# Diagonal blocks that stay in SBUF around a triangular solve, and engine queues re-planned from a table of durations, in a hybrid DeltaNet and attention layer

## The chip, the cores and the metric

The kernel runs on one core of one Trainium2 chip. The metric is the device time of one execution in microseconds; the time of a kernel is the median over several executions. Five queues matter: PE (TensorE, matrix products), DVE (VectorE), ACT (ScalarE), POOL (GpSimd), and SP (SyncE), which in this kernel only issues DMAs. Each engine takes its instructions strictly in the order of its own queue. An instruction whose inputs are not there stops everything behind it on that engine.

## The reference

One layer over 2048 tokens of width 1024, all in fp32. The input is normalised and projected, and the columns of the projection feed two groups of heads. Group A (four heads of 128) is a gated DeltaNet, run forward and backward over the sequence. Group B (eight query heads of 64) is attention in a window of 128 with a sink. Both pass a gate, and one output projection adds the result to the input. What the change touches is the DeltaNet:

```python
m = jnp.where(strict, jnp.einsum('bhncd,bhnsd->bhncs', k_beta, k) * decay, 0.0)
t_inv = lax.linalg.triangular_solve(eye + m, eye, left_side=True, lower=True, unit_diagonal=True)
u = jnp.einsum('bhncs,bhnse->bhnce', t_inv, v * beta[..., None])
...
def step(state, inp):               # scanned over the chunks, forward and backward
    v_new = u_i - jnp.einsum('bhcd,bhde->bhce', w_i, state)
    o = einsum(q_i * exp(g_i), state) + einsum(a_i, v_new)
    state = state * exp(g_last) + einsum(k_dec, v_new)
```

In each chunk and direction a unit triangular matrix is inverted, and the inverses feed a recurrence over the chunks.

## The kernel before

The kernel works in chunks of 128 tokens (16 of them, `NCH`). fp32 operands of the large projections are split into a high and a low fp32r part, so that such a product is three matmuls.

- **Phase A** normalises and transposes the input and runs all projections with the convolution and the attention. Products are `pq_*` (rows), `pf_c*` (convolution) and `pf_z*` (gates); attention products are `s`, `pt`, `po`.
- **Phase B** takes the four DeltaNet heads h = 0 to 3, each in four functions. `pre_front(h)` loads keys and queries of four chunks at a time (`k_q`), transposes them (`tr`, `trv`), forms the products `gh` and writes the scaled triangular matrices `ma` (tiles `ma`, and for some heads `xhi_h` and `xlo_h`). `solve(h)` inverts the 32x32 diagonal blocks of all 16 chunks and both directions at once: each of the 128 partitions holds one block, `L` has the blocks and `X` their inverses, and 31 steps of two dependent DVE instructions each (lines 749 and 753) do the elimination. `invert(h)` builds the 128x128 inverses from the blocks in four groups `hi`, each with five matmul products `pi0` to `pi4`; it places the small inverses in the tiles `iv0` to `iv3` and in `ma`. `scan(h)` is the recurrence: 16 steps, two directions, products `pk`, `py`, `po`, states `S`, and at its end a normalisation (`sso`, `tro`, `zt`) into DRAM (`mix_dn`).
- **Filling work** in phase B is `sw_units`: 32 units `pcs` that project the attention outputs (loads `mxs`, `xrs`, `zcs`, stores `part`). In the end `out_pair` projects the DeltaNet outputs (`pcd`).

The blocks travel between these functions through DRAM. After each group of four chunks, `pre_front` stores the matrices with a DMA to `m_d` (line 716). `solve` loads the diagonal blocks back with two DMAs, `X` for the forward half (line 739) and `L` for the backward half (line 740); DVE copies the forward half into `L` transposed (line 742), and POOL clears `X`. After the last step `X` is stored to `x_d` (line 754). `invert` loads `xc` from there, one DMA for each group and direction (line 765), and DVE transposes 32x32 blocks of it into `xt` (line 766); copies on DVE or POOL (lines 776 and 793) put both in place.

The order of all instructions on each engine is not that of the code. `set_order` builds a graph of dependences over all instructions, gives every instruction a duration (`cost`) and every dependence a delay (`LAG`), and plans the queues by list scheduling, forward and backward in turn, 12 times (`plan`). The plan with the shortest end is written out as the order of each queue. A DMA has a fixed issue time, one landing delay for loads and stores alike (`LAG` of SP) and a transfer time worked out from its pieces; the durations of the other engines come from formulas in the number of elements.

Of the kernel before, what the change touches and what calls it, by code (L numbers as in the profile page):

```python
# [7 lines left out]
F32 = mybir.dt.float32  # L8
# [7 lines left out]
P = 128  # L16
# [530 lines left out]
def phase_b(ctx, wide, xe, ae, late, tc, t, ident, consts, hp, mix_dn, mix_sw, kq_d, v_d, zdn_d, zsw_d, dp, out):  # L547
# [93 lines left out]
    def pre_front(h):  # L641
# [10 lines left out]
        m_d = dp.tile([2, NCH, 4 * (32 * P + 32)], F32, tag="m_d", name=f"m_d{h}", bufs=2)  # L652
        x_d = dp.tile([2, NCH, P, 32], F32, tag="x_d", name=f"x_d{h}", bufs=2)
        for n, c4 in enumerate(FRONT):
# [60 lines left out]
            for d in range(2):  # L715
                dma(m_d[d, s4, : P * P].rearrange("u (i j) -> i u j", j=P), ma[d, c4][:, :, 0])
# [13 lines left out]
        H["solve"] = m_d, x_d, mp  # L730
        return H

    def solve(h, H):
        m_d, x_d, _ = H["solve"]
        L = qa.tile([P, 32, 32], F32, tag="L", name=f"L{h}")
        X = qa.tile([P, 32, 32], F32, tag="X", name=f"X{h}")
        lv = [m_d[d].rearrange("u (p y) -> (u p) y", p=4)[:, : 32 * P] for d in range(2)]
        lv = [a.rearrange("q (r x) -> q r x", x=P)[:, :, :32] for a in lv]
        dma(X[0:64], lv[0])
        dma(L[64:128], lv[1])  # L740
        x = X.rearrange("p r c -> p (r c)")
        V.tensor_copy(L[0:64], X[0:64].rearrange("p r c -> p c r"))
# [11 lines left out]
        dma(x_d.rearrange("d u (p r) c -> (d u p) (r c)", p=4), X.rearrange("p r c -> p (r c)"))  # L754

    def invert(h, H):
        _, x_d, mp = H["solve"]
        for hi in range(4):
# [3 lines left out]
            for d, c4 in ((0, hi), (1, 3 - hi)):  # L762
                xc = qb.tile([P, 4, 32], F32, tag="xc", name=f"xc{h}_{d}_{c4}", bufs=4)
                xt = qb.tile([P, 4, 32], F32, tag="xt", name=f"xt{h}_{d}_{c4}", bufs=4)
                dma(xc, x_d[d, 4 * c4 : 4 * c4 + 4].rearrange("u i c -> i u c"))
                V.transpose(xt.rearrange("p u c -> p (u c)"), xc.rearrange("p u c -> p (u c)"))
                x0[d], x1[d] = (xc, xt) if d == 0 else (xt, xc)
# [277 lines left out]
def set_order(tc):  # L1045
# [371 lines left out]
```

## Time and profile before

| quantity | value |
|---|---|
| median of three timed executions | 1261.1 us |
| lowest and highest of them | 1256.62 and 1261.7 us |
| profiled execution, span from first to last instruction (the only time shown for it) | 1268.0 us |
| mean granted TensorE clock over the span | 0.989 |
| PE busy | 1210.5 us (95%), 7018 instructions |
| DVE busy | 953.7 us (75%), 2320 instructions |
| ACT busy | 725.8 us (57%) |
| POOL busy | 529.2 us (42%) |
| DMA | 206.39 MB, 163 GB/s in the mean |

The profile is of one execution. An instruction row gives start, duration, engine, line, operation, names of output and inputs, shape, and in brackets how long its engine sat idle before it and what ended that. A row of windows gives, for a stretch of time, its length, the busy time of PE, PE's weight load, DVE, ACT and POOL with the number of their instructions, the granted TensorE clock, the share of the DMA engines and GB/s. A fp32 matmul is two PE instructions. The ends of matmuls are modelled, so that a PE that is called busy may still be running below its best rate.

### The profile page before, as it was taken

Reading aid. Unit: us, or ns where it says so; the run is one execution under the profiler, and the core shown is the slowest. Engines: PE = TensorE matmul, PEld = TensorE weight load, DVE = VectorE, ACT = ScalarE, POOL = GpSimd, SP = SyncE. Lnnn points to the kernel's source line nnn. Section 1 sums busy time; section 2 is a strip of 40 time slices with the busy share of each in tenths; the row PEclk is TensorE's granted clock in tenths of the full one; section 3 lists DMA queues with packets and bytes.
Section 4 is the critical chain, followed back from the end, with each engine's and each line's share of the span. In section 5 each row is a group of like instructions: output and inputs, shape, how many; then the busy total and the mean of one; then the engine's idle time right before and its main releaser. Section 6 shows DMA issues by size and latency. Waiting matters only on the chain.

```text
span 1268.0 us, 22351 instructions
## 1 busy us (share of the span) xinstructions
PE 1210.5 (95%) x7018; PEld 1037.4 (82%) x7018; DVE 953.7 (75%) x2320; ACT 725.8 (57%) x2167; POOL 529.2 (42%) x845
## 2 busy tenths in 40 slices
PE   6999999999999999999999998999889899999898
PEld 5998888788889988887777777888789689888776
DVE  4523689999854379999995587698769779876765
ACT  6432476666534367766665438658557845685421
POOL 2243454763302276556422304613742441670541
PEclk9999999999999999999999999999889999999999
DMA  7553243513544434431016848967955875854785
GB/s 259 172 160 125 75 154 100 173 60 102 166 145 125 144 110 137 137 96 55 34 51 207 238 141 245 264 189 207 268 166 174 236 200 152 242 175 122 238 269 199
DMA packets 232294, 206.39 MB, mean 163 GB/s; under 512 B 49137, under 2 KB 181873, under 8 KB 232177
## 3 DMA queue, kind: packets, MB, share of 16 engines
q1 hardware_dynamic: 232176, 204.97, 53.0%
q8 instruction: 56, 0.92, 0.3%
q14 instruction: 62, 0.50, 0.1%
HBM read 139.84 MB, written 65.08 MB: 162 GB/s over the span
## 4 chain that ended last, share of the span: by engine, by line
PE 67%; DVE 13%; DMA 9%; ACT 4%; issue 3%; POOL 1%; SPq 1%; DVEq 0%; ACTq 0%; POOLq 0%
PE pf_c L199 5%; PE pf_c L201 5%; PE pf_c L200 5%; PE pf_z L199 4%; PE pf_z L200 4%; PE pf_z L201 4%; PE pi L781 3%; PE pq_q L212 2%; PE pq_q L211 2%; PE pt L390 2%; PE pq_q L210 2%; DMA xc<-x_d 2%; PE py L830 2%; PE po L839 2%; PE pcs L596 2%
## 5 line engine op out<-in xcount | busy, mean ns | idle before, releaser
L199 PE MATMUL pf_c<-xhi,wh_c 128*128 128x512 f32 x384 | 155.7, 405 | 0.8 <-DVE acc L269 0.8
L200 PE MATMUL pf_c<-xlo,wh_c 128*128 128x512 f32 x384 | 154.7, 403 | 0.0
L201 PE MATMUL pf_c<-xhi,wl_c 128*128 128x512 f32 x384 | 154.3, 402 | 0.0
L269 DVE SCALAR_TENSOR_TENSOR acc<-pf_c,cw,acc 128x512 f32<-128x512 f32 (+1 forms) x192 | 140.8, 742 | 2.6 <-POOL acc L259 0.7
L385 POOL TENSOR_SCALAR pr<-pr,st 128x384 f32<-128x384 f32 (+1 forms) x128 | 79.4, 639 | 98.0 <-DVE st L383 71.2
L394 ACT ACTIVATE ph<-pt 128x512 fp32r<-128x512 f32 x92 | 53.0, 595 | 60.5 <-PE pt L390 51.5
L376 ACT ACTIVATE pr<-pr,st 128x384 f32<-128x384 f32 (+1 forms) x128 | 76.2, 597 | 17.8 <-DVE st L372 17.4
L199 PEld LDWEIGHTS pf_c<-xhi,wh_c 128*128 128x128 f32 x384 | 72.5, 189 | 13.5 <-DVE acc L269 1.3
L201 PEld LDWEIGHTS pf_c<-xhi,wl_c 128*128 128x128 f32 x384 | 72.3, 188 | 12.9
L200 PEld LDWEIGHTS pf_c<-xlo,wh_c 128*128 128x128 f32 x384 | 72.4, 188 | 11.6
L835 ACT ACTIVATE yk<-py,ck 128x128 f32<-128x128 f32 x120 | 43.9, 366 | 62.0 <-PE py L830 61.2
L372 DVE CUSTOM_DVE_ANT_0 pr<-s,mask,sink 128x384 f32<-128x384 f32 (+1 forms) x128 | 73.4, 593 | 2.5 <-PE s L371 1.0
L211 PE MATMUL pq_q<-wh_q,xlo 128*128 128x256 f32 x256 | 72.1, 282 | 0.0
L212 PE MATMUL pq_q<-wl_q,xhi 128*128 128x256 f32 x256 | 71.9, 281 | 0.0
L210 PE MATMUL pq_q<-wh_q,xhi 128*128 128x256 f32 x256 | 71.4, 280 | 0.0
L390 PE MATMUL pt<-ident,pr 128*128 128x128 f32 x368 | 69.5, 274 | 1.8 <-DVE pl L395 1.1
L395 DVE TENSOR_TENSOR pl<-pt,ph 128x512 fp32r<-128x512 f32 x92 | 61.6, 681 | 6.1 <-ACT ph L394 5.6
L390 PEld LDWEIGHTS pt<-ident,pr 128*128 128x128 f32 x368 | 47.8, 140 | 20.4 <-DVE pl L395 4.4
L596 PE MATMUL pcs<-wohs,mhs 128*128 128x512 f32 x128 | 58.3, 456 | 4.4 <-ACT mhs L590 2.7
L692 POOL TENSOR_TENSOR nk<-ssk,pw 128x4 f32<-128x4 f32 x16 | 16.5, 1029 | 106.8 <-DVE ssk L691 106.6
L597 PE MATMUL pcs<-wohs,mls 128*128 128x512 f32 x128 | 56.1, 438 | 1.7 <-DVE mls L591 1.7
L598 PE MATMUL pcs<-wols,mhs 128*128 128x512 f32 x128 | 55.0, 429 | 0.0
(324 smaller groups left out, 4029.4 us busy)
## 6 DMA issues: line engine op xcount, KB each, us to landing
kqc<-kq_d SPq DMA_DIRECT2D x120, 128.0 KB, 3.1
ws_c<-wt SPq DMA_DIRECT2D x48, 256.0 KB, 3.5
xr<-x SPq DMA_DIRECT2D x16, 512.0 KB, 5.3
k_q<-kq_d SPq DMA_DIRECT2D x16, 512.0 KB, 5.6
mxs<-mix_sw SPq DMA_DIRECT2D x32, 256.0 KB, 3.7
xrs<-x SPq DMA_DIRECT2D x32, 256.0 KB, 3.7
part<-xrs SPq DMA_DIRECT2D x32, 256.0 KB, 2.6
xrd<-part SPq DMA_DIRECT2D x32, 256.0 KB, 4.1
```

The source lines that it names most:

```text
L199: T.matmul(ps, hi[:, k, cs], xhi[b][:, k], start=(k == 0), stop=False)
L200: T.matmul(ps, hi[:, k, cs], xlo[b][:, k], start=False, stop=False)
L201: T.matmul(ps, lo[:, k, cs], xhi[b][:, k], start=False, stop=(k == KC - 1))
L210: T.matmul(ps[:, :n], xh, hi[:, k, :n], start=(k == 0), stop=False)
L211: T.matmul(ps[:, :n], xl, hi[:, k, :n], start=False, stop=False)
L212: T.matmul(ps[:, :n], xh, lo[:, k, :n], start=False, stop=(k == KC - 1))
L269: V.scalar_tensor_tensor(av, ps[:, lo:], cw[:, i, k : k + 1], av, ALU.mult, ALU.add)
L372: V.tensor_tensor_reduce(pr[j][:, :n], ps[:, :n], mask[:, lo * P : hi * P], 1.0, sink[:, hh : hh + 1], ALU.add, ALU.min, accum_out=nm[:, j ...
L376: A.activation(pr[j][:, :n], pr[j][:, :n], AF.Exp, bias=nm[:, j : j + 1], scale=-1.0, accum_out=den[:, j : j + 1])
L385: G.tensor_scalar(pr[j][:, :n], pr[j][:, :n], den[:, j : j + 1], 1.0, ALU.mult, ALU.mult)
L390: T.transpose(pt[:, j], pr[j][:, (kb - lo) * P : (kb - lo + 1) * P], ident)
L596: T.matmul(ps, mh[:, k], wh[:, k], start=(k == 0), stop=False)
```

## The change

It has two parts. The first keeps the blocks in SBUF. `pre_front` copies each diagonal block with POOL from `ma` into one of two tiles (`C` and `L`, named `Cg` and `Lg` in the order's rows): 32 copies of 32x128 elements for each head. `solve` transposes the backward half into `C` (512 elements on each partition) and the whole into `L` (1024 elements) with DVE's 32x32 transpose, and after the 31 steps transposes `X` twice (1024 elements each) into `XC` and `XT`, from which `invert` takes slices. The tiles `Cg` and `XC` share one buffer (tag `C`), and `Lg`, `L` and `XT` share another (tag `L`). All DMAs to and from `m_d` and `x_d` are gone.

The second part changes the planner. Durations come from a table of means (`TIMES`, by engine, names and number of elements), transfer times of DMAs from another (`MOVES`); a landing takes `LOAD` for a load into SBUF and `STORE` for a store, plus the transfer. The search runs twice, with a smaller and a larger time spared after every DMA. Candidates are no longer compared by the planned end but by the mean end of three replays (`replay`), in which the queue orders stay fixed, durations vary at random, DMAs land late by a random amount, and 3 in 100 DMA issues take longer. This moves instructions everywhere in the program.

```diff
-        m_d = dp.tile([2, NCH, 4 * (32 * P + 32)], F32, tag="m_d", name=f"m_d{h}", bufs=2)
-        x_d = dp.tile([2, NCH, P, 32], F32, tag="x_d", name=f"x_d{h}", bufs=2)
+        blocks = [qa.tile([P, n, 32], F32, tag=k, name=f"{k}g{h}") for k, n in (("C", 32), ("L", 16))]
...
             for d in range(2):
-                dma(m_d[d, s4, : P * P].rearrange("u (i j) -> i u j", j=P), ma[d, c4][:, :, 0])
+                for q in quads:
+                    G.tensor_copy(blocks[d][q, s4], ma[d, c4][q, :, 0, q])
...
     def solve(h, H):
-        m_d, x_d, _ = H["solve"]
+        C, B = H["solve"][0]
+        V.transpose(C[:, NCH:].rearrange("p u r -> p (u r)"), B.rearrange("p u r -> p (u r)"))
         L = qa.tile([P, 32, 32], F32, tag="L", name=f"L{h}")
         X = qa.tile([P, 32, 32], F32, tag="X", name=f"X{h}")
-        lv = [m_d[d].rearrange("u (p y) -> (u p) y", p=4)[:, : 32 * P] for d in range(2)]
-        lv = [a.rearrange("q (r x) -> q r x", x=P)[:, :, :32] for a in lv]
-        dma(X[0:64], lv[0])
-        dma(L[64:128], lv[1])
+        V.transpose(L, C.rearrange("p u r -> p r u"))
         x = X.rearrange("p r c -> p (r c)")
-        V.tensor_copy(L[0:64], X[0:64].rearrange("p r c -> p c r"))
...
-        dma(x_d.rearrange("d u (p r) c -> (d u p) (r c)", p=4), X.rearrange("p r c -> p (r c)"))
+        XC = qa.tile([P, 32, 32], F32, tag="C", name=f"XC{h}")
+        XT = qa.tile([P, 32, 32], F32, tag="L", name=f"XT{h}")
+        V.transpose(XC.rearrange("p u c -> p c u"), X.rearrange("p r c -> p c r"))
+        V.transpose(XT.rearrange("p u r -> p r u"), X)
+        H["solved"] = XC, XT
...
             for d, c4 in ((0, hi), (1, 3 - hi)):
-                xc = qb.tile([P, 4, 32], F32, tag="xc", name=f"xc{h}_{d}_{c4}", bufs=4)
-                xt = qb.tile([P, 4, 32], F32, tag="xt", name=f"xt{h}_{d}_{c4}", bufs=4)
-                dma(xc, x_d[d, 4 * c4 : 4 * c4 + 4].rearrange("u i c -> i u c"))
-                V.transpose(xt.rearrange("p u c -> p (u c)"), xc.rearrange("p u c -> p (u c)"))
+                u = slice(NCH * d + 4 * c4, NCH * d + 4 * c4 + 4)
+                xc, xt = XC[:, u], XT[:, u]
...
-LAG = {"PE": 205, "DVE": 140, "Activation": 160, "Pool": 120, "SP": 2400}
+LAG = {"PE": 205, "DVE": 140, "Activation": 160, "Pool": 120}
+LOAD, STORE = 2050, 1350
+TIMES = {
+    "ACT acc<-pf_c 512": 591, "ACT al<-al 8": 108, "ACT b<-pi 512": 488, "ACT beta<-bd 128": 227,
...
+MOVES = {
+    "L<-m_d": 1749, "X<-m_d": 1137, "csk<-cs": 199, "csq<-cs": 188, "dc<-dec": 849, "dc<-gr_d": 811, "dec<-gm": 646,
...
+        known = TIMES.get(f"{dict(Activation='ACT', Pool='POOL').get(eng, eng)} {pair(i)} {m}")
+        if known:
+            return known
...
+            move[k] = MOVES.get(pair(insts[k][0]), count / piece * (8 + 0.148 * piece) / 16)
+            inside = a.tensor.name in tiles and "DRAM" not in str(tiles[a.tensor.name].space)
+            land[k] = LOAD if inside else STORE
...
-    for i in range(12):
-        if i < 8:
-            stretch(*now[1:])
-        back = plan([-(b + d) for b, d in zip(now[1], dur)], False)
-        now = plan([-(b + d) for b, d in zip(back[1], dur)], True)
-        if i >= 7 and (best is None or now[0] < best[0]):
-            best = now
+    best = None
+    for spare in (300, 600):
+        slow = [0.0] * total
+        now = plan([k - 1e9 if k < stage else -rank[k] for k in range(total)], True, spare)
+        for i in range(14):
+            if i < 8:
+                stretch(now[1], now[2])
+            back = plan([-(b + d) for b, d in zip(now[1], dur)], False, spare)
+            now = plan([-(b + d) for b, d in zip(back[1], dur)], True, spare)
+            if i > 7:
+                end = sum(replay(now[2], seed) for seed in range(3)) / 3
+                if best is None or end < best[0]:
+                    best = end, now[1], now[2]
```

In the order's rows below, the digit after a name is the head, the next one the direction or the group, and the last one the step or the chunk; the long number is the buffer. Line numbers after the change differ by a few from those before.

The first place is DVE at the end of `solve(1)`, where `tm1_30` and the last `X1` are its 31st step, `r0`, `S0` and `oacc0` belong to the scan of head 0, and `iv0` and `iv2` are tiles that `invert(1)` fills. Before, the row that first uses the result, `xt1_0_0`, stands 26 rows after the last `X1`:

```order
L749 TENSOR_TENSOR tm1_30_10372<-L1_10275,X1_10276 128x31
L694 TENSOR_TENSOR bp2_11356<-beta_4894,ssk2_11354 128x2x4
L842 SCALAR_TENSOR_TENSOR S0_0_14_9676<-S0_0_13_9636,egt_4922,po0_0_14_9668 128x128
L753 TENSOR_TENSOR X1_10276<-X1_10276,tm1_30_10372 128x31
L711 SCALAR_TENSOR_TENSOR ma2_0_11512<-gh2_0_0_11548,bp2_11356,v2_q_7736 128x2x128
L823 SCALAR_TENSOR_TENSOR r0_0_15_9705<-pk0_0_15_9703,negc_4920,vs0_3_8017 128x128
L842 SCALAR_TENSOR_TENSOR S0_1_14_9696<-S0_1_13_9656,egt_4922,po0_1_14_9688 128x128
L858 SCALAR_TENSOR_TENSOR oacc0_3_9091<-po0_0_14_9668,egc_4924,oacc0_3_9091 128x128
```

After the change the same place reads:

```order
L748 TENSOR_TENSOR tm1_30_10389<-L1_10294,X1_10295 128x31
L861 TENSOR_TENSOR oacc0_2_9246<-po0_0_9_9416,oacc0_2_9246 128x128
L752 TENSOR_TENSOR X1_10295<-X1_10295,tm1_30_10389 128x31
L860 SCALAR_TENSOR_TENSOR oacc0_1_9225<-po0_1_9_9436,egc_4924,oacc0_1_9225 128x128
L755 STREAM_TRANSPOSE XC1_10392<-X1_10295 128x32x32
L756 STREAM_TRANSPOSE XT1_10393<-X1_10295 128x32x32
L778 COPY iv0_0_8795<-XC1_10392 32x4x32
L778 COPY iv0_0_8795<-XT1_10393 32x4x32
L778 COPY iv0_0_8795<-XC1_10392 32x4x32
L778 COPY iv0_0_8795<-XT1_10393 32x4x32
L778 COPY iv2_0_8798<-XC1_10392 32x4x32
```

The two transposes and the first copies of `invert(1)` now stand right behind the last step, and beside step 10 of the scan of head 0 instead of step 14.

The second place is PE at the border between the scans of heads 0 and 1, where `py1_0_0` is the first product of the new scan, `pi0_1` and `pi4_1` are products of `invert(1)`, and `pcs10` is filling work. Before, 40 rows stand between the last product of the old scan (`po0_1_15`) and `py1_0_0`; these are the last of them:

```order
L887 MATMUL tro0_0_9755<-ident_66,oacc0_0_9078 128x128
L887 MATMUL tro0_3_9768<-ident_66,oacc0_3_9091 128x128
L781 MATMUL pi4_1_0_10436<-xlo_h_9050,iv1_0_8771 128x128 x4
L887 MATMUL tro0_3_9768<-ident_66,oacc0_3_9091 128x128 x3
L781 MATMUL pi0_1_1_10465<-iv0_1_8770,g1_1_10451 128x128 x2
L596 MATMUL pcs10_0_11718<-wohs0_10071,mhs10_0_11712 128x512
L781 MATMUL pi0_1_1_10465<-iv0_1_8770,g1_1_10451 128x128
L830 MATMUL py1_0_0_10644<-vs1_0_9993,xlo_h_9050 128x128
L781 MATMUL pi0_1_1_10465<-iv0_1_8770,g1_1_10451 128x128
```

After the change:

```order
L834 MATMUL po0_0_15_9702<-S0_0_14_9670,kqc0_0_15_9695 128x128
L850 MATMUL po0_0_15_9702<-y0_0_15_9705,ma0_3_7912 128x128
L834 MATMUL po0_1_15_9717<-S0_1_14_9690,kqc0_1_15_9710 128x128
L850 MATMUL po0_1_15_9717<-y0_1_15_9720,ma0_3_7912 128x128
L832 MATMUL py1_0_0_10632<-vs1_0_10005,xlo_h_9044 128x128
L783 MATMUL pi0_1_3_10587<-iv0_1_8796,g1_3_10573 128x128
L783 MATMUL pi4_1_2_10566<-xhi_h_9043,iv1_0_8797 128x128
```

Now `py1_0_0` follows `po0_1_15` directly, and `invert(1)` is already in its last two groups (`hi` 2 and 3), where it was in its first two before.

The third place is SP around the loads of `solve(2)`, where `kqc1_0_5` is the load for step 5 of the scan of head 1. Before:

```order
L583 DMA mxs11_0_11733<-mix_sw11_82 128x512
L593 DMA xrs10_0_11716<-x 128x512
L586 DMA zcs11_0_11735<-zsw_d_99 128x4x128
L739 DMA X2_11866<-m_d2_11359 64x32x32
L740 DMA L2_11865<-m_d2_11359 64x32x32
L819 DMA kqc1_0_5_10832<-kq_d1_88 128x2x128
L819 DMA kqc1_1_5_10852<-kq_d1_88 128x2x128
L600 DMA part10_7723<-xrs10_0_11716 128x512
L889 DMA zt1_1_11181<-zdn1_96 128x512
L819 DMA kqc1_0_6_10872<-kq_d1_88 128x2x128
L889 DMA zt1_2_11194<-zdn1_96 128x512
```

After the change, around the same load:

```order
L893 DMA mix_dn_100<-zt0_3_9767 128x512
L821 DMA kqc1_0_5_10820<-kq_d1_88 128x2x128
L821 DMA kqc1_1_5_10840<-kq_d1_88 128x2x128
L602 DMA part9_7722<-xrs9_0_11702 128x512
L891 DMA zt1_1_11169<-zdn1_96 128x512
L891 DMA zt1_2_11182<-zdn1_96 128x512
L595 DMA xrs10_0_11728<-x 128x512
L588 DMA zcs11_0_11747<-zsw_d_99 128x4x128
L585 DMA mxs11_0_11745<-mix_sw11_82 128x512
L821 DMA kqc1_0_6_10860<-kq_d1_88 128x2x128
L821 DMA kqc1_1_6_10880<-kq_d1_88 128x2x128
```

The two loads from `m_d` are gone from the queue, and with them the wait of `L2` for the stores to `m_d`; the loads `xrs` and `zcs`, the stores `part` and the loads of the scan follow one another without it.

More of the change, by code (lines that the diff above doesn't have):

```diff
@@ L753, in solve @@
             V.tensor_tensor(X[:, c + 1 :, 0 : c + 1], X[:, c + 1 :, 0 : c + 1], tv, ALU.subtract)
-        dma(x_d.rearrange("d u (p r) c -> (d u p) (r c)", p=4), X.rearrange("p r c -> p (r c)"))
+        XC = qa.tile([P, 32, 32], F32, tag="C", name=f"XC{h}")
[3 more added lines that the diff above has]
+        H["solved"] = XC, XT
     def invert(h, H):
-        _, x_d, mp = H["solve"]
+        mp = H["solve"][1]
+        XC, XT = H["solved"]
         for hi in range(4):
@@ new lines @@
+MOVES = {
+    "L<-m_d": 1749, "X<-m_d": 1137, "csk<-cs": 199, "csq<-cs": 188, "dc<-dec": 849, "dc<-gr_d": 811, "dec<-gm": 646,
+    "gm<-gr_d": 1490, "k_q<-kq_d": 1947, "k_q<-v_d": 675, "kq_d<-acc": 1361, "kqc<-kq_d": 368, "kv<-kv_d": 346,
+    "kv_d<-sgkv": 356, "kw<-kw": 590, "m_d<-ma": 749, "m_d<-xhi_h": 732, "m_d<-xlo_h": 741, "mix_dn<-zt": 660,
+    "mix_sw<-ot": 346, "mxd<-mix_dn": 369, "mxs<-mix_sw": 657, "out<-xrd": 651, "part<-xrs": 654, "q_d<-sgq": 354,
+    "ql<-q_d": 634, "qw<-qw": 420, "v_d<-acc": 1342, "v_q<-dec": 680, "v_q<-gr_d": 920, "wos<-wout": 656,
+    "woss<-wout": 669, "ws_c<-wt": 684, "ws_kv<-wkv": 350, "ws_q<-wq": 672, "ws_z<-wt": 1120, "x_d<-X": 1246,
+    "xc<-x_d": 291, "xr<-x": 1307, "xrd<-part": 666, "xrs<-x": 693, "xt<-xT": 1323, "zc<-zsw_d": 361,
+    "zcs<-zsw_d": 812, "zdn<-zo": 663, "zs<-wt": 385, "zsw_d<-zo": 666, "zt<-zdn": 709,
+}
@@ L1226, in set_order @@
     eng = [e for _, e in insts] + [None] * (total - n)
-    move, late = [0.0] * total, [0.0] * total
+    moves = [k < n and "DMA" in str(insts[k][0].opcode) for k in range(total)]
+    move, land = [0.0] * total, [0.0] * total
     nxt, prv = [[] for _ in range(total)], [[] for _ in range(total)]
     for k in range(total):
-        if eng[k] == "SP":
+        if moves[k]:
             a = aps(insts[k][0].outs)[0]
@@ L1279, in stretch, with plan @@
             slow[k] = (slow[k] + t + need - begin[k] - dur[k]) / 2
-    def plan(order, forward):
+    def plan(order, forward, spare):
         to, back = (nxt, prv) if forward else (prv, nxt)
@@ L1344, in set_order @@
     stage = min(used[x][0] for x in used if x.startswith("L0_"))
-    now, best = plan([k - 1e9 if k < stage else -rank[k] for k in range(total)], True), None
-    for i in range(12):
-        if i < 8:
-            stretch(*now[1:])
-        back = plan([-(b + d) for b, d in zip(now[1], dur)], False)
-        now = plan([-(b + d) for b, d in zip(back[1], dur)], True)
-        if i >= 7 and (best is None or now[0] < best[0]):
-            best = now
+    best = None
[11 more added lines that the diff above has]
+                    best = end, now[1], now[2]
     end, begin, queue = best
```

125 lines of the change are left out of this document (107 added, 18 removed), and 9 rows, old and new, of the table TIMES.

## The prediction, made before the changed kernel ran

> **What bounds the kernel now.** I read the page first (the busy times), then busy time by stage (windows), then PE's idle times in the timeline, then the chain that ended last at those places, and last the rows of the tiles that the change removes.
>
> ```profile
> span 1268.0 us, 22351 instructions
> PE 1210.5 (95%) x7018; PEld 1037.4 (82%) x7018; DVE 953.7 (75%) x2320; ACT 725.8 (57%) x2167; POOL 529.2 (42%) x845
> ...
> core 0: us, PE busy (x) PEld busy (x) DVE busy (x) ACT busy (x) POOL busy (x), PEclk, DMA share, GB/s
> 0.00:28.00 28.00, 16.89 (x104) 15.29 (x104) 14.33 (x25) 16.29 (x34) 7.15 (x21) 1.00 0.74 247
> 160.00:320.00 160.00, 159.29 (x780) 130.74 (x778) 152.31 (x320) 104.66 (x242) 88.79 (x135) 1.00 0.36 118
> 480.00:680.00 200.00, 197.28 (x988) 159.43 (x988) 192.40 (x437) 137.45 (x347) 106.90 (x161) 1.00 0.29 96
> 680.00:760.00 80.00, 77.25 (x362) 62.28 (x361) 50.83 (x138) 37.85 (x146) 14.09 (x13) 1.00 0.65 185
> 760.00:800.00 40.00, 35.52 (x197) 29.43 (x196) 32.01 (x95) 29.58 (x118) 21.57 (x45) 0.96 0.85 247
> 800.00:884.00 84.00, 79.88 (x559) 71.86 (x558) 67.85 (x215) 59.51 (x229) 26.91 (x37) 1.00 0.75 215
> 884.00:913.00 29.00, 22.99 (x128) 19.64 (x128) 22.36 (x67) 17.25 (x73) 18.82 (x42) 0.88 0.95 276
> 913.00:994.00 81.00, 75.97 (x530) 69.39 (x530) 66.50 (x205) 56.13 (x223) 31.25 (x41) 0.96 0.65 189
> 994.00:1025.00 31.00, 25.66 (x149) 21.42 (x149) 23.53 (x75) 20.14 (x79) 17.79 (x41) 0.94 0.83 222
> 1025.00:1097.00 72.00, 69.53 (x481) 62.91 (x480) 60.42 (x191) 40.64 (x137) 23.09 (x49) 0.98 0.62 181
> 1097.00:1177.00 80.00, 76.67 (x560) 68.96 (x559) 59.49 (x161) 53.42 (x188) 37.43 (x53) 1.00 0.58 170
> 1177.00:1268.00 91.00, 82.55 (x358) 64.84 (x357) 59.28 (x99) 26.62 (x74) 36.50 (x41) 1.00 0.73 236
> ```
>
> PE is the bound, with 57.5 us idle in all. The change takes no matrix product away, so it can only win PE's idle time, its time at a lower clock, and time in which it runs slowly though called busy. Of the idle time, 11.1 us lie in the first 28 us, behind the first loads, whose order both kernels fix. The stretches 160 to 320 and 480 to 680 (convolution and attention) have PE over 98% busy and DVE at 95 and 96%: two full engines, where no order can win much. From 680 on the DeltaNet heads run. The scans fill 800 to 884, 913 to 994, and 1025 on; between them lie two stretches, 884 to 913 and 994 to 1025, where PE is busy for 23.0 of 29 us and 25.7 of 31 us and its clock is 0.88 and 0.94. PE's idle times there, and the chain:
>
> ```profile
> 891.45 1.03 PE L702 MATMUL gh<-k_q 128*128 128x256 f32 x4
> 896.11 2.05 PE L781 MATMUL pi<-iv,g 128*128 128x128 f32 x8 [3.64 <-DVE iv L776]
> ...
> 934.11 0.80 PE L821 MATMUL pk<-S,kqc 128*128 128x128 f32 x2 [3.24 <-DVE S L842]
> ...
> 896.00:902.00 6.00, 5.20 (x20) 4.67 (x21) 5.02 (x18) 3.17 (x10) 4.94 (x13) 0.50 0.92 245
> 933.00:940.00 7.00, 5.89 (x22) 5.41 (x23) 5.33 (x14) 2.18 (x6) 6.06 (x14) 0.51 0.42 129
> ...
> 882.43 6.82 DMA x_d<-X
> 889.27 4.05 DMA xc<-x_d
> ...
> 989.96 6.23 DMA x_d<-X
> 996.21 7.61 DMA xc<-x_d
> ...
> 1004.15 0.10 DVE iv L776
> ```
>
> So the chain between two scans is the way of the inverses through DRAM: 10.9 us at 882 and 13.8 us at 990. And a PE that stood still for over 3 us then runs at half clock for 6 or 7 us, so that such a hole costs about double.
>
> **The change, part by part.**
>
> *The way back from the solve.* Removed for each head: one store of `X`, eight loads `xc`, eight transposes. Added: two transposes of 1024 elements.
>
> ```profile
> 881.82 0.18 DVE L753 TENSOR_TENSOR X<-X,tm 128x31 f32<-128x31 f32 x1
> 893.58 0.17 DVE L776 COPY iv<-xc 32x128 f32<-32x128 f32 x1
> ...
> L742 DVE COPY L<-X x4: 1096/1114/1120, 729.8 to 1026.6; 64x1024 f32<-64x1024 f32 x4
> L766 DVE STREAM_TRANSPOSE xt<-xc x32: 270/311/314, 779.4 to 1109.8; 128x128 f32<-128x128 f32 x32
> L776 POOL COPY iv<-xc x48: 279/287/817, 782.5 to 1133.5; 32x128 f32<-32x128 f32 x48
> ```
>
> From the last step to the first `iv` it takes 11.6 us now (882.0 to 893.6). No row has a transpose of 1024 elements. From below it costs as a copy of 1024 elements, 1.11 us; from above as eight transposes of 128, 2.49 us. The two then take 2.2 to 5.0 us; I take 3.0 (1.5 each), nearer the copy, since part of the 311 ns must be a fixed cost (a copy of 128 elements, at 893.58, took 170 ns). The path shortens by about 8.5 us for each head. [...]
>
> *The way to the solve.* Removed for each head: eight stores to `m_d`, the two loads `X` and `L`, the copy of line 742. Added: 32 POOL copies and two transposes (512 and 1024 elements).
>
> ```profile
> 903.81 0.47 DVE L711 SCALAR_TENSOR_TENSOR ma<-gh,bp,dc 128x256 f32<-128x256 f32 x1
> 914.49 3.90 SPq L740 DMA_DIRECT2D L<-m_d  x1
> 923.05 1.10 DVE L742 COPY L<-X 64x1024 f32<-64x1024 f32 x1
> 924.46 0.38 SPq L593 DMA_DIRECT2D xrs<-x  x1
> 925.88 0.22 DVE L753 TENSOR_TENSOR X<-X,tm 128x31 f32<-128x31 f32 x1
> 931.41 0.69 DVE L599 TENSOR_TENSOR xrs<-xrs,pcs 128x512 f32<-128x512 f32 x1 [4.23 <-DMA xrs<-x]
> 932.58 1.21 DVE L753 TENSOR_TENSOR X<-X,tm 128x112 f32<-128x112 f32 x1
> ...
> 932.31 1.35 POOL L587 TENSOR_TENSOR mxs<-mxs,zcs 128x512 f32<-128x512 f32 x1 [3.99 <-DMA zcs<-zsw_d]
> ```
>
> From the last `ma` (904.3) to the first step (925.9) 21.6 us pass. Afterwards it is the last eight POOL copies (8 x 0.287 = 2.3 us) and the two transposes, 1.5 times the price above, 1.7 to 3.7 us, so about 5 us: some 16 us earlier. There is a second gain: SP stood for 3.9 us at `L<-m_d` until the stores had landed, and everything behind it, among it the load `xrs` issued at 924.46, came that much later. DVE waited for this load (4.23 us), `S` stood behind it on DVE, and PE waited for `S`: the hole of 3.24 us at 934. The wait goes with the DMA. What is late next is a load behind one of the scan's own `kqc` waits, which the trace shows without a hole of PE of this size.
>
> *Sum for PE.* Idle time and lost clock together (length minus busy, plus length times the missing clock) are 2.75 us in 680 to 760, 4.5 + 1.6 in 760 to 800, 4.1 in 800 to 884, 6.0 + 3.5, 5.0 + 3.2, 5.3 + 1.9, 2.5 + 1.4, and 3.3 in 1097 to 1177: 45 us. The best a stretch with a scan shows is 3.3 in 80 (4%); 1025 to 1097 has 3.9 in 72 (5.4%). With 5.4% left everywhere, 760 to 800 gives 4 us, 884 to 913 gives 8, 913 to 994 gives 4 and 994 to 1025 gives 5.5: 21.5 us. In addition the invert and scan products interleave more evenly, as the order shows. PE issued 559 instructions in 84 us (6.65 per us) in the first scan and 560 in 80 (7.0) in the last; the 1847 instructions from 800 to 1097 take 278 us at the first rate and 264 at the second, instead of 297. The lower rate gives 19 us there, the higher 33; I add 6 us to the 21.5, between the two, so 27.5.
>
> *What the new work costs.* DVE: 3.5 transposes of 1024 at 1.5 us, less 8 x 0.311 and 1.1, is 1.7 us more for each head (bounds 0.3 and 5.1). DVE is 76 to 84% busy in the stretches from 800 to 1097, so part shows: 2 us in all (bounds 0 and 15). POOL: 128 x 0.287 = 36.7 us, on an engine that is busy for 118 of 297 us there; hidden by its idle time, but a DVE instruction with two SBUF inputs can be caught: the `X` step of 932.58 took 1.21 us while POOL ran `mxs`, where the smaller step at 925.88 took 0.22. Block copies stand mostly ahead of the solve, where DVE reads PSUM; I take 1 us (bounds 0 and 10). [...]
>
> *The planner elsewhere.* It re-orders everything before 680 and after 1177. PE's idle time from 28 to 680 is small and DVE is full; I take 1.5 us gained (bounds: 5 gained, 10 lost, the latter a twentieth of DVE's 200 us at 480 to 680). After 1177 the way from `zt` through DRAM to `pcd` is unchanged: nothing.
>
> Sum: 27.5 - 3 + 1.5 = 26 us. The span of the profiled execution, 1268.0, lies 6.9 us (0.5%) above the median of the runs, 1261.1; 1268.0 - 26 = 1242 for an execution like it, and 1261 - 26 = **1235 us** for the median.
>
> **The rivals.**
>
> *The shared buffers turn the solve and the invert into one chain (slower).* `XC` and `Cg` share one buffer, `XT`, `L` and `Lg` another, each single. The copies for head h+2 can't start before `invert(h+1)` has read its last slice; before, they overlapped:
>
> ```profile
> 948.47 0.55 POOL L776 COPY iv<-xt 32x128 f32<-32x128 f32 x1
> ```
>
> `invert(1)` read from 893.6 to 949, 55 us, and `solve(2)` had started at 925.9. The solve then took 64 us (to 990). At these lengths a head would need 55 + 64 = 119 us, plus some 9 us of block copies and 5 to 8 us of transposes: 133 us, against 110.6 from one first `iv` to the next now (893.58 to 1004.15). Even if only 6 us of that excess showed for two heads, the time would be 1261 + 12 - 6 (the other gains) = 1267. It decides at 110 us for reading, copies, transposes and solve together. Against it: in the order, the PE rows from the first product of `invert(1)` to the last that its reading waits for fall from 137 to 58 (head 2: 178 to 71), and the DVE rows in the solve from 176 to 110 (167 to 135). That is room of a third, so 8 in 100.
>
> *The latency was half hidden.* The scans end earlier but DVE, which is over 80% busy in them, becomes the pace: then only the two stretches of PE idling shrink by half (8 us) and the rate stays: 1261 - 8 = 1253. For it speaks DVE's 83.9% at 1025 to 1097; against it that just this stretch has little idle PE. 14 in 100.
>
> *POOL's copies hold DVE.* Were half of the 128 copies each to hold a DVE instruction for its 0.287 us, as `mxs` held the `X` step, that is 18 us instead of the 1 taken, and 1252. Against it: the `ma` instructions, beside which most copies stand, read `gh` from PSUM. 4 in 100. [...]
>
> *The planner wins on top.* If phase B runs at 7.0 instructions per us throughout (33 us), 760 to 800 gives 4 and phase A its 5, it is 42 less 1 to 3: 1221, and less if the end too gets denser. 17 in 100.
>
> *Nothing that can be measured,* since PE's work is the same and holes reappear elsewhere: 1259, 4 in 100.
>
> **How the numbers follow.** The forecast, 1226 to 1246, has 53 in 100. The range 1209 to 1257 takes in most of the dense case, the half-hidden one and POOL's copies, and leaves out the slower chain and no change. A measurement of this kernel can tell about 0.5% (6 us) from no change. Faster by more than that: 53 + 17 + 12 of the 18 for the half-hidden case and POOL's copies = 82; within it: 6 + 4 = 10; slower: 8.
>
> **What would show it.** Right: no idle PE over 2 us and no half clock between the scans; the first `iv` within 4 us of the last `X` step; the first `X` step within 8 us of the last `ma`; no wait of DVE for `xrs` over 3 us; a transpose of 1024 elements of 1.1 to 1.9 us; from 800 on about 7 PE instructions per us. Wrong: block copies on POOL waiting for products of `invert` (the shared buffers), `X` steps of over 0.5 us beside POOL copies, or a PE that waits for DVE in 160 to 680.

## The result: 1293.2 us, slower, and the profile after

| kernel | median of its runs, us | ratio to the kernel before, 95% interval |
| --- | --- | --- |
| before | 1261.1 (1256.6 to 1261.7) | 1 |
| changed | 1293.2 (1291.7 to 1296.1) | 1.0268 [1.0237, 1.0299] |

The change costs 32 us where 26 were forecast as a gain. The two profiled executions lie only 22.7 us apart (1268.0 and 1290.7), because that of the kernel before was longer than its timed ones; the traces can account for these 22.7. The head of the page and the same stretches as before, by busy time (start and end, length, then busy microseconds and instructions of each engine, the granted clock, the DMA share):

```profile
span 1290.7 us, 22358 instructions
PE 1217.0 (94%) x7018; PEld 1042.4 (81%) x7018; DVE 966.7 (75%) x2300; ACT 728.8 (56%) x2167; POOL 566.6 (44%) x973
...
480.00:680.00 200.00, 195.10 (x970) 159.29 (x969) 187.63 (x429) 135.32 (x339) 111.35 (x160) 0.98 0.26 88
...
760.00:800.00 40.00, 36.19 (x219) 31.27 (x218) 25.68 (x65) 24.09 (x86) 24.85 (x64) 1.00 0.27 83
800.00:884.00 84.00, 74.96 (x466) 65.10 (x466) 74.04 (x210) 50.64 (x191) 34.32 (x71) 0.96 0.65 198
884.00:913.00 29.00, 28.38 (x218) 25.80 (x217) 20.99 (x68) 25.94 (x114) 23.29 (x56) 1.00 0.57 169
913.00:994.00 81.00, 67.78 (x429) 57.82 (x427) 69.23 (x198) 45.51 (x173) 31.70 (x53) 0.98 0.60 181
994.00:1025.00 31.00, 30.94 (x246) 29.14 (x244) 22.81 (x72) 28.79 (x128) 23.09 (x52) 1.00 0.53 170
1025.00:1097.00 72.00, 66.07 (x430) 57.78 (x429) 62.13 (x193) 47.09 (x175) 18.16 (x36) 0.98 0.53 166
1097.00:1177.00 80.00, 71.09 (x489) 64.14 (x488) 60.48 (x153) 45.41 (x147) 42.97 (x74) 0.96 0.53 165
```

The two stretches between the scans, whose holes the forecast wanted to fill, are full: PE is busy for 28.4 of 29 us (23.0 before) and 30.9 of 31 (25.7 before). But in the stretches of the solves PE has lost more: 75.0 against 79.9, 67.8 against 76.0, 66.1 against 69.5, 71.1 against 76.7. Taken as one stretch, before and after:

```profile
800.00:1177.00 377.00, 350.71 (x2397) 314.17 (x2396) 300.14 (x911) 247.07 (x924) 155.27 (x262) 0.97 0.69 199
```

```profile
800.00:1177.00 377.00, 339.22 (x2265) 299.79 (x2264) 309.69 (x888) 243.38 (x919) 173.52 (x338) 0.97 0.57 177
```

PE got through 2265 instructions instead of 2397. The 132 that are missing are 21 us at the rate of before (2397 in 377 us), nearly all of the 22.7 us between the two spans.

Why the solves starve PE is seen where the buffers are handed on. First DVE's rows from the last step of `solve(1)` to the first copy of `invert(1)`; then, from POOL, the places where `invert(0)`, `invert(1)` and `invert(2)` read their last slices (`iv`) and the blocks of the next head (`Cg`) are written:

```profile
868.98 0.18 DVE L752 TENSOR_TENSOR X<-X,tm 128x31 f32<-128x31 f32 x1
869.34 2.18 DVE L755 STREAM_TRANSPOSE XC<-X 128x1024 f32<-128x1024 f32 x1
871.43 1.88 DVE L756 STREAM_TRANSPOSE XT<-X 128x1024 f32<-128x1024 f32 x1
873.17 0.18 DVE L778 COPY iv<-XC 32x128 f32<-32x128 f32 x1
```

```profile
799.93 0.29 POOL L718 COPY Cg<-xhi_h 32x128 f32<-32x128 f32 x1
800.26 0.29 POOL L778 COPY iv<-XT 32x128 f32<-32x128 f32 x1
...
904.91 0.28 POOL L718 COPY Cg<-ma 32x128 f32<-32x128 f32 x1
905.89 0.29 POOL L778 COPY iv<-XT 32x128 f32<-32x128 f32 x1
...
1020.27 0.29 POOL L718 COPY Cg<-xlo_h 32x128 f32<-32x128 f32 x1
1020.60 0.29 POOL L778 COPY iv<-XT 32x128 f32<-32x128 f32 x1
```

Each time the first block of the next head is written while the last slices are being read, not earlier: reads, block copies, transposes, solve, transposes, reads have become one chain. The trace, read head by head (from the first to the last copy out of `XC` or `XT`, before out of `xc` or `xt`; then the first read of the last head, and the time from it to the end of the span):

| kernel | reads of heads 0, 1, 2, us | first read of head 3 | from there to the end |
| --- | --- | --- | --- |
| before | 52, 55, 59 | 1086.3 | 181.7 |
| changed | 32, 35, 34 | 1108.1 | 182.6 |

So what follows the last head's first read is as long as before, and the 22 us are all gone by then. These are the rows of that read, of before and of after:

```profile
1086.28 0.40 DVE L776 COPY iv<-xc 32x128 f32<-32x128 f32 x2
```

```profile
1108.14 1.27 POOL L795 COPY xhi_h<-XC 32x128 f32<-32x128 f32 x4 [4.14 <-DVE XC L755]
```

The last head shows the lost overlap best. Before, the `X` steps of `solve(3)` (1035 to 1077) ran for 28 of their 42 us beside the reads of `invert(2)` (1004 to 1063). After the change those reads take 987 to 1021, the blocks of head 3 are written from 1020 to 1049, and the `X` steps run from 1053 to 1105.

And PE during `solve(1)`, in the changed kernel and in the one before (their `X` steps ran from 833 to 869 and from 823 to 882):

```profile
833.00:869.00 36.00, 31.84 (x185) 26.26 (x183) 33.80 (x111) 13.93 (x44) 0.94 (x1) 1.00 0.55 173
```

```profile
823.00:882.00 59.00, 56.53 (x394) 50.49 (x393) 53.04 (x177) 40.88 (x168) 14.22 (x14) 1.00 0.67 197
```

DVE is no freer than before: it is busy for 33.8 of 36 us, 21 of them with the solve's own steps. But the work of other heads that fed PE beside the solve is gone. Before, 118 of the 394 PE instructions were products of `invert(0)` (62 `pi`) or of a front (20 `gh`, 24 `tr`, 12 `trv`); after, six are (2 `pi`, 4 `tr`). What is left for PE is the scan and the filling work `pcs`: 5.1 instructions per us instead of 6.7, 88% busy instead of 96%.

### The profile page after: what moved, and what is told of

Its sections match the earlier page's. It is cut to its first block, busy times and chain, and to the rows that moved or that the text cites. A ratio compares the mean times of both kernels' runs of the same rounds, so it can differ in the third digit from the quotient of the medians.

```text
span 1290.7 us, 22358 instructions
## 1 busy us (share of the span) xinstructions
PE 1217.0 (94%) x7018; PEld 1042.4 (81%) x7018; DVE 966.7 (75%) x2300; ACT 728.8 (56%) x2167; POOL 566.6 (44%) x973
## 5 line engine op out<-in xcount | busy, mean ns | idle before, releaser
L271 DVE SCALAR_TENSOR_TENSOR acc<-pf_c,cw,acc 128x512 f32<-128x512 f32 (+2 forms) x192 | 140.8, 745 | 3.9 <-ACT acc L267 2.9
L589 POOL TENSOR_TENSOR mxs<-mxs,zcs 128x512 f32<-128x512 f32 x16 | 20.9, 1306 | 74.1 <-DMA zcs<-zsw_d 31.4
```

Source lines behind the costliest of these rows:

```text
L271: V.scalar_tensor_tensor(av, ps[:, lo:], cw[:, i, k : k + 1], av, ALU.mult, ALU.add)
```

## Experiments

Ratios are to runs of the kernel before on the same chip. "Old planner" is the planner of before, "over DRAM" its way of the blocks. Theory R: the shared buffers cost. Theory S: the way inside SBUF costs, whatever its part. Theory T: the transposes and copies cost. Theory P: the new planner costs. Theory Z: any new plan moves the time.

### Each part alone

The new code of front, solve and invert under the old planner:

> The first part of the change alone: blocks stay in SBUF, the queues are planned by the planner of before (its formulas, one landing delay, shortest planned end). Theory P (the new plan is worse, the SBUF way is sound): 1235 to 1255 us, the gaps between scans nearly gone. Theory S (the SBUF way itself costs: four transposes of 0.7 to 2.2 us each head in one piece on DVE, 128 POOL copies, the shared buffers): 1275 to 1295 us, like the whole change. If both share it: about 1265.

The old code under the new planner:

> The second part alone: the kernel of before with its way through DRAM, planned by the new tables and replays. Theory P: 1285 to 1305 us, slower than before, with the same hole of PE near 600 to 640 us and the scans over 100 us long. Theory S: 1245 to 1262 us, not slower than before.

The changed kernel with its new instructions added to the table of durations:

```
+    "DVE Cg<-Lg 512": 700, "DVE L<-Cg 1024": 2000, "DVE XC<-X 1024": 2100, "DVE XT<-X 1024": 1880,
+    "POOL Cg<-ma 128": 288, "POOL Lg<-ma 128": 288, ...
```

> The whole change, with the durations measured in its own profile put into the table for the instructions that it lacks: transposes 700, 2000, 2100 and 1880 ns (the planner's formula gives about 650 to 1220), block copies 288 ns (the formula gives 200). Theory D (the new instructions are planned too short, so that DVE blocks the scan): 1255 to 1275 us. Theory P or S: within 1280 to 1300 us.

Measured: 1285.9 us (1.0195 [1.0157, 1.0234]), 1274.8 (1.0101 [1.0069, 1.0134]) and 1289.9 (1.0232 [1.0181, 1.0282]). Both parts are slower alone. The second fell between the bands of P (from 1285) and S (to 1262) and so decides neither. The missing durations are at most a small share: the changed kernel's 1.0268 lies within the interval of the third run.

### What a new plan alone is worth

Before one can blame the planner, one has to know what laying the kernel out anew does. The kernel before, with one number of its planner changed by 1 and by 2 ns:

```
-LAG = {"PE": 205, "DVE": 140, ...
+LAG = {"PE": 205, "DVE": 141, ...
```

> The kernel before with one number of the planner changed by 1 ns (what it adds after a DVE instruction: 141 instead of 140), so that the same instructions are laid out anew. It measures how much a new plan alone moves the time. Theory P (the new planner's rules are worse): re-planning by the old rules is worth nothing, 1257 to 1266 us. Theory Z (any new plan of this kernel lands somewhere in a band of 10 us or more): 1250 to 1280 us, away from 1261 by more than 5.

> The kernel before with the same number at 138. Theory P: 1257 to 1266 us. Theory Z: 1250 to 1280 us, and another value than at 141.

Measured: 1272.2 us (1.0104 [1.0077, 1.0132]) and 1274.6 (1.0124 [1.0092, 1.0157]). The same instructions in another order cost 13.5 and 15.9 us (two values that can't be told apart); the plan of before is a good one among its neighbours. Theory Z holds, and the new planner's 1.0101 over DRAM can't be told from it. Where the 13 us lie the traces don't show: the profiled execution of before (1268.0) was longer than its timed ones, and as long as that of the first of these (1269.0).

Then the new planner's durations and landings without its reserve after a transfer, and with the plan chosen by its own end, as before:

```
-    for spare in (300, 600):
+    for spare in (0,):
-                end = sum(replay(now[2], seed) for seed in range(3)) / 3
+                end = now[0]
```

> The way over DRAM with the new planner's durations and landings, but without the reserve after a transfer, and the plan chosen by its own end as before instead of by the replay. If the replay and the reserve made the new planner worse (1274.8 us): 1258 to 1266 us. If the durations or the landings made it worse: 1270 to 1280 us. Theory Z: anywhere from 1255 to 1285 us, which tells nothing of the two.

Measured: 1295.2 us (1.0286 [1.0233, 1.0339]), 10 us above even the band of Theory Z. The replay and the reserve don't make the new planner slow; without them its plan was 20 us slower. One plan, in a band this wide, says no more of the replay; but it is a plan over DRAM, with no shared buffer, that is as slow as the changed kernel.

### The buffers set free

`Cg`, `Lg`, `XC` and `XT` each get a buffer of their own (10 KB of each partition more), paid for by one buffer less for `kqc`, `oacc`, `y`, `yk`, `jko`, `g` and `b1`. Two controls have only the smaller pools.

```
-        blocks = [qa.tile([P, n, 32], F32, tag=k, ...) for k, n in (("C", 32), ("L", 16))]
+        blocks = [qa.tile([P, n, 32], F32, tag=k, ...) for k, n in (("Cg", 32), ("Lg", 16))]
-        XT = qa.tile([P, 32, 32], F32, tag="L", name=f"XT{h}")
+        XT = qa.tile([P, 32, 32], F32, tag="XT", name=f"XT{h}")
```

> Both ways inside SBUF with the old planner (as in the run of 1285.9 us), but the blocks of front, the transposed blocks, X's two transposes each have a buffer of their own, 10 KB more, paid for by one buffer less for kqc, oacc, y, yk, jko, g and b1. All transposes and POOL copies stay. Theory R: 1255 to 1266 us, equal to the control over DRAM with the same smaller pools. Theory T: 1280 to 1290 us, as with shared buffers.

> Control: both ways inside SBUF with the shared buffers and the old planner, and the same smaller pools as the ring-free kernel (kqc, oacc, y, yk, jko, g, b1 one buffer less). Both theories: 1283 to 1300 us, that is 1285.9 us plus what the smaller pools cost.

> Control: the kernel before with the same smaller pools, nothing else. Both theories: 1258 to 1268 us, the smaller pools cost little. Over 1275 us would say that the pools matter by themselves and the ring-free run has to be read against this one.

Free buffers with the new planner:

> The changed kernel, its planner included, with the solve's buffers each on its own and one buffer less for kqc, oacc, y, yk, jko, g and b1 (as in the ring-free run). Theory R (the shared buffers cost): 1293 less the 16 to 32 us that the ring cost under the old planner, that is 1262 to 1278 us, near the 1274.8 us of the new planner with the way over DRAM. Theory T (transposes and copies): 1285 to 1300 us.

Free and shared buffers, laid out anew with the old planner:

> The ring-free kernel (both ways inside SBUF, own buffers, smaller pools, old planner), laid out anew by the same 1 ns change of the planner (141). If the way inside SBUF is worth what the forecast gave it once its buffers are free (27 us against a newly laid out kernel before, 1272 to 1275 us): 1245 to 1255 us. If the latencies were hidden already: 1265 to 1278 us, the same band as the newly laid out kernels over DRAM.

> The same at 138. Gain as forecast: 1245 to 1255 us. Latencies hidden already: 1265 to 1278 us.

> Shared buffers (both ways inside SBUF, old planner, full pools) at 141. Theory R: 1283 to 1303 us whatever the plan, as in the four shared plans run so far (1286 to 1301 us). Theory Z (those four were only bad draws): 1265 to 1280 us.

| planner, pools | over DRAM | SBUF, free buffers | SBUF, shared buffers |
| --- | --- | --- | --- |
| old, full pools | 1; 1.0104; 1.0124 | | 1.0195; 1.0154 [1.0124, 1.0184] |
| old, smaller pools | 1.0058 [1.0031, 1.0084] | 1.0036 [1.0018, 1.0055]; 1.0102 [1.0067, 1.0137]; 1.0007 [0.999, 1.0024] | 1.0286 [1.0246, 1.0325] |
| new | 1.0101 | 1.0103 [1.0059, 1.0147] | 1.0268; 1.0232 |
| new, without replay and reserve | 1.0286 [1.0233, 1.0339] | | |

In every row that has them the shared buffers are slowest: 1.0154 and more, against 1.0103 and less with free ones. Only the plan over DRAM in the last row is as slow, so one bad plan can cost as much as the sharing. In the new planner's row, the sharing is 1.0268 - 1.0103, or 21 us. Other pairs give other sizes: 1.0286 against 1.0036 is 32 us, and at 141 1.0154 against 1.0102 is 7 us (there the free plan has the smaller pools).

Between free buffers and DRAM no row shows a difference: a mean of 1.0048 against 1.0058, and 1.0103 against 1.0101. With plans of the same number there is none at 141 (1.0102 against 1.0104) and 15 us at 138 (1.0007 against 1.0124, with full pools). So a gain of a few microseconds is neither shown nor excluded.

In the order of the texts above, the seven took 1269.6, 1301.3, 1273.5, 1272.2, 1273.4, 1260.5 and 1277.3 us. Not all fell where they were expected. The first three lie 1 to 6 us above the bands of Theory R or of both theories, on a chip on which the kernel before took 1266.3. The shared plan at 141 (1277.3 us) lies under the band of Theory R and in that of Theory Z, though above all free plans. The free one at 138 (1260.5) lies between the band of a hidden latency (from 1265) and that of the forecast gain (to 1255). It equals the kernel before (1.0007); no kernel that computes the whole reference was faster than that one.

The ring-free trace (1265.9 us) shows the overlap restored. POOL's first block for head 1, and its first and last group of copies for `invert(0)`:

```profile
773.38 0.63 POOL L718 COPY Cg<-xhi_h 32x128 f32<-32x128 f32 x2 [9.29 <-DVE xhi_h L712]
...
781.57 0.93 POOL L795 COPY ma<-XC 32x128 f32<-32x128 f32 x3
...
847.83 1.73 POOL L795 COPY ma<-XT 32x128 f32<-32x128 f32 x4
```

and PE during its `solve(1)`, by busy time:

```profile
821.00:867.00 46.00, 45.34 (x324) 41.73 (x324) 42.46 (x135) 27.84 (x101) 12.85 (x28) 1.00 0.51 153
```

The blocks begin 8 us ahead of the reads; the reads stretch over 68 us (781.6 to 849.6), into the solve, and feed PE there: 7.0 instructions per us and 99% busy.

### Part of the way, part of the sharing

The way to the solve inside SBUF, the way back over DRAM (one store in four pieces, eight loads), with one buffer less for `kqc`, `y`, `yk` and `jko`:

> Only the way to the solve stays inside SBUF (block copies on POOL, two transposes per head); the way back goes over DRAM as before (one store in four pieces per head, eight loads of xc), with the old planner and one buffer less for kqc, y, yk and jko. The buffers of the solve are then free again as soon as it has stored X, so no block copy and no solve has to wait for the products of the head ahead. Theory R (the shared buffers chain solve of head h+1 to the products of head h): about 1262 us, 1255 to 1268, since the chain is gone. Theory T (the long strided transposes on DVE and the copies on POOL are what costs): the transposes left are 2.8 of 6.9 us a head, so some 40 to 50% of the 25 us stay: about 1272 us.

Only the chain from the products to the next head cut (`Cg` shares with `X`, `Lg` and `XT` have their own):

```
-  ... for k, n in (("C", 32), ("L", 16))]
+  ... for k, n in (("X", 32), ("Lg", 16))]
```

> Only the chain from the products to the next head's blocks and factors is cut: the blocks of front share their buffer with X (free as soon as the solve ahead has ended), the transposed blocks and X's two transposes have their own; kqc, oacc, y and yk have one buffer less. Theory R: 1263 to 1278 us, as ring-free, because no instruction of the solve or front waits for the products of the head ahead. If a chain from the blocks to the solve ahead costs as much: 1283 us and over.

Measured: 1280.4 us (1.011 [1.0054, 1.0166]; the kernel before ran at 1266.3 on that chip) and 1267.9 (1.0079 [1.0048, 1.0109]). The second is as Theory R said: sharing with `X` costs nothing that can be told from a new plan, so it is the sharing with `XC` and `XT` that costs. The first was expected at 1262 or 1272 and decides nothing: 1.011 is what a new plan costs over DRAM.

### Waits or order, and the transposes

The free buffers, with the planner told that they are shared; each row of each engine is then that of the shared kernel with the smaller pools:

```
+    for chain in (("Cg", "XC"), ("Lg", "L", "XT")):
+        line = [named[f"{k}{h}"] for h in range(4) for k in chain]
+        for x, y in zip(line, line[1:]):
+            gate(x, y)
```

> The ring-free kernel, with the planner told as if the buffers were still shared: every engine's row is then that of the shared kernel with the same small pools (1301.3 us), instruction for instruction, while the buffers are free. If the sharing costs through waits on the chip: 1265 to 1275 us, as ring-free. If it costs through the order that it imposes on the rows: 1296 to 1304 us.

Plain copies in place of the three transposes of 1024 elements, in the same order, with shared and with free buffers:

```
-        V.transpose(L, C.rearrange("p u r -> p r u"))
+        V.tensor_copy(L, C)
...
-        V.transpose(XC.rearrange("p u c -> p c u"), X.rearrange("p r c -> p c r"))
-        V.transpose(XT.rearrange("p u r -> p r u"), X)
+        V.tensor_copy(XC, X)
+        V.tensor_copy(XT, X)
```

> Both ways inside SBUF with shared buffers and the old planner (1285.9 us), every row in the same order, but the three transposes of 1024 elements per head (2.0 to 2.2 us each) are plain copies of the same buffers, about 0.6 to 1.1 us each: the transposing itself is left out. Theory T (the long transposes are on the path): 3 to 5 us less per head, 12 to 18 us in all, 1268 to 1274 us. Theory R: less than 5 us, 1281 to 1286 us.

> The same exchange of transposes for copies (the transposing is left out) in the ring-free kernel at 138 (1260.5 us), every row in the same order. If the transposes eat what the way inside SBUF gains: 1245 to 1252 us. If they lie beside other work there: 1256 to 1261 us.

Measured: 1299.9 us (1.0303 [1.0284, 1.0323]), 1275.2 (1.0118 [1.0095, 1.014]) and 1256.4 (0.9966 [0.995, 0.9982]).

The first settles how the sharing costs. With free buffers in the shared order the time stays (1.0303, shared 1.0286), where the free order had 1.0036. So waits for a buffer at run time are not the cost; the planner had put the instructions in an order that honours the chain, and with the buffers free the engines still ran it at that pace: 2153 PE instructions from 800 to 1177, against 2155 with shared buffers and 2445 in the free order. Rows of 800 to 1177, first shared, then free in the shared order:

```profile
800.00:1177.00 377.00, 330.01 (x2155) 288.33 (x2154) 309.55 (x853) 235.30 (x883) 169.02 (x337) 0.98 0.57 173
```

```profile
800.00:1177.00 377.00, 334.52 (x2153) 292.85 (x2152) 306.70 (x852) 235.18 (x882) 168.93 (x337) 0.96 0.56 173
```

The copies for transposes gave about 10 us with shared buffers (1.0195 to 1.0118), just above what T said, and about 5 with free ones (1.0007 to 0.9966). The groups of the run with shared buffers (busy time, then the mean of one in ns):

```profile
L740 DVE COPY L<-Cg 128x1024 f32<-128x1024 f32 x4 | 3.5, 868 | 0.1
...
L756 DVE COPY XT<-X 128x1024 f32<-128x1024 f32 x4 | 2.8, 694 | 0.0
L755 DVE COPY XC<-X 128x1024 f32<-128x1024 f32 x4 | 2.8, 691 | 0.1
```

In the transposing kernel these take 2045, 1940 and 2155 ns, so a loop of the chain gets 3.9 us shorter. The last head's first read stands after the first solve and three loops, 15.6 us of shorter instructions: it came at 1089.9 instead of 1103.4 us, and the span was 1272.1 instead of 1285.1. So T and R are one thing here: with shared buffers the transposes are links of the chain, and 10 to 13 of the 15.6 us show; with free buffers 5 do.

## Why the prediction was wrong

*The rival of the shared buffers was right, and its price and chance were the failed step.* It was given 8 in 100 and 1267 us. The forecast took the opposite for granted: that "the invert and scan products interleave more evenly, as the order shows", at 6.65 to 7.0 PE instructions per us. By the same five rows from 800 to 1097 PE got through 1789 in 297 us, 6.0 per us, fewer than the 1847 of before (6.2). The rival's condition was a loop of over 110 us; measured from first read to first read the loops are 102.6, 115.2 and 121.3 us (769.0, 871.6, 986.8, 1108.1), where before they were 113.9, 110.5 and 82.2. The chance was cut because rows of PE and DVE between the links became fewer, "room of a third". For two heads the room was there: reads took 32 and 35 us instead of 52 and 55, the solves behind them 36 and 47 instead of 59 and 63; but the last solve grew from 42 to 52. And the block copies, put at some 9 us, take 27 to 29, since they follow the `ma` of the whole of front and stood behind the reads of the head ahead; and a shorter solve is a solve without other work beside it. The rows that went missing between the links were PE's food during the solve. A row count in an order told how close the links stand, not what the engines do meanwhile.

*The two holes closed, the sum for PE did not hold.* 884 to 913 and 994 to 1025 gave 5.4 and 5.3 us of busy PE and, with the clock back at 1.00, 8.9 and 7.1 us in all, against 8 and 5.5 in the sum. The step that failed is that the best share, 5.4%, would hold everywhere: PE was idle for 9.0 of 84, 13.2 of 81 and 8.9 of 80 us in the scans. Nor were the holes between scan and scan all gone: waits of 1.85 us at 874 and 2.60 us at 1028 had half clock behind them (rows in the last section). With free buffers, too, no gain of the size of the forecast is seen. That the latency was hidden by other work, the second rival's reason, fits this, but no run shows it by itself.

*The ways themselves came as forecast.* From the last `X` step to DVE's first `iv` it takes 4.0 us for head 1 (869.2 to 873.2), 4 as said and 11.6 before. From the last `ma` to the first step of head 1:

```profile
824.89 0.48 DVE L712 SCALAR_TENSOR_TENSOR xlo_h<-gh,bp,dc 128x256 f32<-128x256 f32 x1
...
829.21 0.71 DVE L737 STREAM_TRANSPOSE Cg<-Lg 128x512 f32<-128x512 f32 x1 [0.26 <-POOL Lg L718]
...
830.07 2.07 DVE L740 STREAM_TRANSPOSE L<-Cg 128x1024 f32<-128x1024 f32 x1
...
832.95 1.06 DVE L752 TENSOR_TENSOR X<-X,tm 128x31 f32<-128x31 f32 x1
```

7.6 us, under 8 as said; over the four heads it is 7.6 to 9.7, and 17.0 to 25.1 before. DVE's long wait for `xrs` is gone too (0.4 us in all of the kernel). So the path is some 20 us shorter per head, and yet no gain is seen, with free buffers either. That PE was bound by this path for little of the time is the likely reason; it is argued, not shown.

*The transposes* took 1.9 to 2.2 us, not 1.5 (a sign of being right was 1.1 to 1.9); together with 0.71 for the one of 512 elements a head pays 6.9 us of DVE, less 3.6 saved, 3.3 instead of 1.7. The bounds of 0 to 15 us for DVE's cost hold the 10 us (5 with free buffers) that came out for transposes against plain copies; the 2 us taken were too few.

```profile
L755 DVE STREAM_TRANSPOSE XC<-X 128x1024 f32<-128x1024 f32 x4 | 8.7, 2168 | 0.0
L740 DVE STREAM_TRANSPOSE L<-Cg 128x1024 f32<-128x1024 f32 x4 | 8.2, 2046 | 0.0
L756 DVE STREAM_TRANSPOSE XT<-X 128x1024 f32<-128x1024 f32 x4 | 7.8, 1950 | 0.0
L737 DVE STREAM_TRANSPOSE Cg<-Lg 128x512 f32<-128x512 f32 x4 | 2.8, 711 | 5.4 <-POOL Lg L718 5.4
```

*The planner elsewhere* was put at 1.5 us gained (bounds 5 gained, 10 lost). A change of 1 ns in the old planner already lost 13.5: the time of one plan had been taken for the time of the rules. In the changed kernel PE lost 2 us of busy time at 480 to 680 (195.1 of 200 us, 197.3 before); a PE that waits for DVE there was one of the signs named for being wrong. *POOL's copies* held no `X` step: all block copies end before the first of them. Nor did they lengthen the `ma`: the 128 DVE instructions that read `gh` took 0.46 to 0.49 us each, 0.44 to 0.49 before. The first step in the rows above took 1.06 us, where the last, of the same size, took 0.18 (868.98); the first ran beside another POOL instruction with two inputs (`dc`, 1.33 us from 832.61), as the forecast had read of `mxs`. That those inputs were the reason no run shows. The end, counted from the first read of the last head, was as long as before (182.6 against 181.7 us).

So the 32 us are about 13 for a new plan (13.5 and 15.9 in the controls, 13.5 with the new planner over DRAM) and about 20 for the shared buffers, taken from the new planner's row; in the other pairs the sharing costs 7 and 32 us. What stays open is why the plan of before is better than its neighbours, and why the size of the sharing's cost changes so much with the plan.

## What to carry to other kernels

A buffer that two stages share is also an order: where a planner fixes the order of the queues, sharing can turn overlap into a chain even if no instruction ever waits for the buffer (here 1.0303 with free buffers in the shared order, 1.0036 in the free one), so count what ran beside what before saving a few KB. Taking some 20 us per head off a path gave no gain here. The likely reason, argued and not shown, is that it pays only in the time for which the bounding engine has nothing else to do; fill the holes on paper and then ask which stretch the filling work was taken from. And where the order comes from a planner, measure a meaningless change of its numbers first: here it was worth 1%, about as much as the parts under test.

## What the runs showed of the hardware

The transposes took longer with more elements, and longer still where the elements lay apart. With the elements side by side, one took 0.311 us for 128 of them (`xt<-xc`, before, the median) and 0.711 us for 512 (`Cg<-Lg`, after). That is 1.04 ns for each further element, and from these two an estimated 1.24 us for 1024. With elements 128 bytes apart on one side, 1024 took 1.95 us (`XT<-X`) and 2.05 us (`L<-Cg`), and on both sides 2.17 us (`XC<-X`): 0.71 to 0.93 us more than that estimate. Plain copies of 1024 elements side by side took 0.69 us (`XC<-X`, `XT<-X`) and 0.87 us (`L<-Cg`) in the run with shared buffers; the copy of before with a strided side took 1.11 us, on 64 partitions. So that row was the wrong neighbour, a strided copy for a strided transpose. That the strides make the difference is an inference: no run here varied the stride alone, and none has a transpose of 1024 elements side by side.

PE's clock halved after shorter holes than the 3 us named in the prediction (1.85 and 2.60 us), and stayed full after a longer one (3.50 us). Two of PE's rows of the changed kernel, with their wait, and the clock beside them (1.00 is full):

```profile
874.39 2.05 PE L783 MATMUL pi<-iv,g 128*128 128x128 f32 x8 [1.85 <-DVE iv L778]
...
1027.97 1.65 PE L703 MATMUL gh<-k_q 128*128 128x256 f32 x3 [2.60 <-DVE xlo_h L712]
```

```profile
874.00:881.00 7.00, 5.92 (x27) 5.66 (x28) 6.75 (x17) 1.82 (x5) 6.07 (x16) 0.51 0.06 22
1028.00:1031.00 3.00, 3.00 (x10) 2.64 (x11) 0.86 (x3) 2.48 (x10) 2.76 (x9) 0.50 0.64 187
```

Waits of 1.9 and 2.6 us were followed by 7 and 3 us at half clock. But in the ring-free kernel a wait of 3.5 us was followed by full clock:

```profile
747.57 0.50 PE L201 MATMUL pf_z<-xhi,zhi 128*128 128x512 f32 x1 [3.50 <-ACT zhi L242]
```

```profile
747.00:754.00 7.00, 5.87 (x26) 4.28 (x27) 5.68 (x19) 4.38 (x13) 0.00 (x0) 1.00 0.27 82
```

In the changed kernel itself a hole of 2.81 us, ahead of `pi` at 789.99, was also followed by 7 us at 1.00 (789.99 to 797). So the length of a hole alone doesn't tell whether the clock halves; what decides it these runs don't show.
